# Rotary turn of queries and keys by two products and accumulating transfers, with the far scores one step later

## The chip, the cores and the metric

The kernel runs on one core of a Trainium2 chip. The metric is the device time in microseconds of one execution; the time before is the median of three runs. The profile shows one execution; its span goes from the first to the last instruction.

## The reference, cut to what matters

One decoder layer: 512 tokens, model width 1024, float32. A wide projection gives queries, keys and values for three groups of 8 heads of 64, the input of a state-space recurrence, and gate logits. Queries and keys are turned by position (rotary), then three causal attentions with different dilations run and are merged by their softmax denominators; the recurrence runs beside them, and the two are gated, projected, normalised and followed by a SwiGLU and a second normalisation.

```python
def apply_rope(t, pos):
    half = HEAD_DIM // 2                      # 32
    inv_freq = ROPE_THETA ** (-jnp.arange(half, dtype=jnp.float32) / half)
    ang = pos[:, None] * inv_freq[None, :]
    cos = jnp.cos(ang)[None, :, None, None, :]
    sin = jnp.sin(ang)[None, :, None, None, :]
    t1 = t[..., :half].astype(jnp.float32)
    t2 = t[..., half:].astype(jnp.float32)
    return jnp.concatenate([t1 * cos - t2 * sin, t1 * sin + t2 * cos], axis=-1)
...
proj = x @ w_in[layer]
q = apply_rope(q, pos)
k = apply_rope(k, pos)
for g, (window, dilation) in enumerate(((128, 1), (512, 4), (2048, 16))):
    o_g, lse_g = dilated_group_attention(q[:, :, g], k[:, :, g], v[:, :, g], window, dilation)
wts = jax.nn.softmax(jnp.stack(lses, axis=0), axis=0)
attn = jnp.sum(wts[..., None] * jnp.stack(outs, axis=0), axis=0)
```

## The kernel before

Each float32 product on TensorE (PE) is made as three products of rounded parts: both operands are split into a high and a low part, and `mm3` issues high x high, high x low and low x high (lines 202 to 204). Weights come from HBM as raw blocks of 1 MB through SP's queue; each half block is split by ACT (`whi`, line 195) and VectorE (DVE; `wlo`, line 196). The class `Weights` keeps three pairs of split buffers: after each step `w.release()` hands one back and splits the next half block into it.

The projection is a list of 56 steps (`STEPS`), each one weight half block against all 512 tokens: 24 matmuls of 128x512. The order is: the recurrence's input (steps 0 to 3), group 0's values (4 to 7), six pairs of gate tiles (8 to 19), group 0's keys (20 to 23) and queries (24 to 27), group 1's values, keys and queries (28 to 31, 32 to 35, 36 to 39), group 2's first two key tiles (40, 41), first two query tiles (42, 43), values (44 to 47), last two key tiles (48, 49), last two query tiles (50, 51), and the last four gate tiles (52 to 55). Then come the GLU of the recurrence's output (56 to 59), the branch projections (60 to 67), the output projection, the feed-forward part and the normalisations.

Other work is laid between by hand: `at_step(n, ...)` puts a function into the middle of step n (after the fourth of eight slices, through `mid`), and `n + 0.5` at its end, after `w.release()`. The engines' instruction queues are filled in exactly this order; nothing is reordered later.

A key or query step (`qk_tile`) makes one tile of 128 rows, two heads of 64, by 512 tokens. `hp` is the tile's number in its group, 0 to 3. Each tile is turned on DVE straight from PSUM: a shuffle inside each block of 32 partitions (`sw`), a product with the cosines (`cq`), a product of `sw` with the signed sines, and the sum into the tile of the group (`dv`). For this the columns of the weights are permuted on the host, so that the partner of each row lies 16 partitions away in the same block of 32. Group 0's tiles are stored with the tokens in another order (`as_phases`).

The attention is done for four pairs of heads, and twice: kind 0 (near: group 0) and kind 1 (far: groups 1 and 2 together). `SCORES[kind]` and `WEIGHTS[kind]` give the places. For pair j, `attn_scores` (PE products at line 806, then for each block a mask and row minimum on DVE, line 817, and the exponential on ACT, line 819) stands at `SCORES[kind][j]`; `attn_turn` (PE transposes of the weights at line 829 and ACT copies at line 831) at `WEIGHTS[kind][j]`; `attn_values` (line 840 and ACT's copy of the result) at `SCORES[kind][j + 1]`. The far scores of pair hp read tile hp of the queries and keys of groups 1 and 2. Functions put at the same place run in the order in which they were put there: values first, then scores.

Around the end stand `merge_sel` (52), `merge_weights` (54: the shares of the near and far kind from their row minima and sums), `split_y` (54.5: the recurrence's output split for the GLU, four casts on ACT and four differences on DVE), `merge_turn` (55.5: PE transposes of the shares), and `merge_pair(hp)` at 58 to 61. The tile pool `at` gives the tags `sw` and `cq` two buffers of 512 floats each; besides the turn, the recurrence's GELU (`y2`), the GLU's gate (`th`) and the merged pair (`a1`) use them. PSUM banks: projection tiles go round banks 0 to 2, scores and turned weights round 3 to 6, values use 7.

POOL (GpSimd) has only memsets and some work of the normalisations; before the change it issues no transfer at all.

Of the kernel before, what the change touches and what calls it, by code (L numbers as in the profile page):

```python
# [10 lines left out]
F32 = mybir.dt.float32  # L11
# [3 lines left out]
ALU = mybir.AluOpType  # L15

P = 128
# [6 lines left out]
NH = 8  # L24
# [21 lines left out]
NLAST = 4  # L46


SCORES = [[30, 33.5, 37, 40, 43.5], [43.5, 48.5, 51.5, 53, 55.5]]
WEIGHTS = [[32, 35.5, 38.5, 42], [45, 50, 52.5, 54]]  # L50

# [3 lines left out]
def by_phase(z):  # L57
    return z.rearrange("p (r c) -> p r c", r=4)


def as_phases(z):

    return z.rearrange("p (c r) -> p r c", r=4)
# [35 lines left out]
class Weights:  # L99
# [58 lines left out]
    def flush(self):  # L158
        if self.after:
            self.after()  # L160
            self.after = None
# [6 lines left out]
def emit(ctx, tc, i, out):  # L168
    nc = tc.nc
    pe, dve, act, pool, sp = nc.tensor, nc.vector, nc.scalar, nc.gpsimd, nc.sync  # L170
# [47 lines left out]
    at = pa_ctx.enter_context(tc.tile_pool(name="at", bufs=2))  # L218
# [12 lines left out]
    def gat(n, name, dt=F32):  # L231
        return pa.tile([P, 2048], dt, tag=f"gat{n}", name=name)
# [4 lines left out]
    w = Weights(nc, wp, split)  # L237
    out_homes = deque(("g0", 2, 6, 3))
    w.add(None, 8)
    for n in range(2, N_GLU, 2):  # L240
        kind, g, un, _ = STEPS[n]
# [61 lines left out]
    rope = pr.tile([P, 2, 512], F32, tag="rope", name="rope")  # L303
# [23 lines left out]
    def ts(o, a, s1, op0, s2=None, op1=None, eng=dve):  # L327
        if s2 is None:
            eng.tensor_scalar(o, a, s1, None, op0=op0)
        else:  # L330
            eng.tensor_scalar(o, a, s1, s2, op0=op0, op1=op1)

    def stt(o, a, s1, b, op0, op1, eng=dve):
        eng.scalar_tensor_tensor(o, a, s1, b, op0=op0, op1=op1)

    def tt(o, a, b, op, eng=dve):
        eng.tensor_tensor(o, a, b, op=op)  # L337
# [196 lines left out]
    ssm = {}  # L534
# [165 lines left out]
    def ssm_out(rnd):  # L700

        if rnd == 0:
            late.take(1000)
            ssm["ysb"] = gat(0, "ysb").rearrange("p (a i b c) -> p a i b c", a=2, i=4, b=2)
        ut, h, y = ssm["ut"], ssm["h"], ssm["ysb"]
        tb, cb = ([ring_(f"y{n}{rnd}{e}").rearrange("p (o i c) -> p o i c", o=2, i=2) for e in range(2)]
                  for ring_, n in ((scores, "t"), (turned, "c")))
        for e in range(2):
            for par in range(2):
                for half, rows in halves64:  # L710
                    for x, cols in halves64:
                        i_ = 4 * rnd + 2 * e + x
                        pe.matmul(tb[half][cols, par, e], ssm["tm"][rows, 2 * i_ + par, :], ut[rows, 2 * i_ + par, :],
                                  start=True, stop=True)
        for e in range(2):
            for half in range(2):
                for r in range(2):
                    for par, rows in halves64:
                        for x, cols in halves64:
                            i_ = 4 * rnd + 2 * e + x  # L720
                            pe.matmul(cb[par][cols, half, e], caf[rows, i_, r, half, :], h[r][rows, 2 * i_ + half, :],
                                      start=(r == 0), stop=(r == 1))
        is_ = slice(2 * rnd, 2 * rnd + 2)
        yf = [y[:, half, is_].rearrange("p i b c -> p (i b c)") for half in range(2)]
        y2 = [at.tile([P, 512], F32, tag="sw", name=f"y2_{rnd}{half}") for half in range(2)]
        for half in range(2):
            for par in range(2):
                act.copy(y[:, half, is_, par], tb[half][:, par])
                tt(y[:, half, is_, par], y[:, half, is_, par], cb[par][:, half], ALU.add)
        for a, b in zip(y2, yf):  # L730
            act.square(a, b)
            ts(a, a, 0.044715, ALU.mult, 1.0, ALU.add)
            tt(a, a, b, ALU.mult)
        for a, b in zip(y2, yf):
            act.activation(a, a, AF.Tanh, scale=math.sqrt(2.0 / math.pi))
            stt(b, a, 1.0, b, ALU.add, ALU.mult)
# [17 lines left out]

    def qk_tile(dv, ws, g, hp, name, mid):
        b = proj_tile(ws, f"p{name}{hp}", mid)
        sw = at.tile([P, 512], F32, tag="sw", name=f"sw{name}{hp}")
        cq = at.tile([P, 512], F32, tag="cq", name=f"cq{name}{hp}")
        dve.stream_shuffle(sw, b, list(range(16, 32)) + list(range(16)))
        tt(cq, b, rope[:, 0, :], ALU.mult)  # L760
        tt(sw, sw, rope[:, 1, :], ALU.mult)
        if g == 0:
            tt(as_phases(dv[:, hp, :]), by_phase(cq), by_phase(sw), ALU.add)
        else:
            tt(dv[:, hp, :], cq, sw, ALU.add)

    def v_tiles(dv, ws, j, g, mid):

# [81 lines left out]
    merged = {}  # L850
# [46 lines left out]
    def merge_pair(hp):  # L897
        if hp == 0:
            for j, n in (("g1", "h"), (1, "l")):
                merged[n] = home(j, f"at{n}", F32R).rearrange("p (q t) -> p q t", q=4)  # L900
        wb = [pairs_(f"wb{hp}{k}") for k in range(2)]
        for kind in range(2):
            pe.matmul(wb[kind], merged["sel"][:, kind, hp, :], merged["w"], start=True, stop=True)
        tt(oa[1][:, hp, :], oa[1][:, hp, :], wb[1], ALU.mult)
        a1 = at.tile([P, 512], F32, tag="cq", name=f"a1{hp}")
        tt(a1, oa[0][:, hp, :], wb[0], ALU.mult)
        tt(a1, a1, oa[1][:, hp, :], ALU.add)
        hi, lo = merged["h"][:, hp, :], merged["l"][:, hp, :]
        act.copy(hi, a1)
        pending.append(lambda: tt(lo, a1, hi.bitcast(F32), ALU.subtract))  # L910
# [64 lines left out]
    for kind in range(2):  # L975
        for j, n in enumerate(SCORES[kind]):
            if j > 0:
                at_step(n, attn_values, kind, j - 1)
            if j < NPAIR:
                at_step(n, attn_scores, kind, j)  # L980
                at_step(WEIGHTS[kind][j], attn_turn, kind, j)
    xn = []
# [34 lines left out]
    for n in range(4, N_GLU):  # L1017
        kind, g, un, c = STEPS[n]
# [6 lines left out]
        else:  # L1025
            if un == 0 and c == 0:
                dv = home({"k": (1, "g3", "g0"), "q": (8, 2, 1), "v": (3, "g1", 0)}[kind][g], f"{kind}{g}")
# [3 lines left out]
            dv = qkv[g]["qkv".index(kind)]  # L1031
# [10 lines left out]
    for n in range(4):  # L1042
        ws = w.views[N_GLU + n]
        bs = []
        for e in range(2):
            b = glu(f"gl{n}{e}")
            co = slice(128 * e, 128 * e + 128)
            for k in range(4):
                mm3(b, (ws[0][:, k, co], ws[1][:, k, co]), (gluin["y"][0][:, k, :], gluin["y"][1][:, k, :]), k == 0, k == 3)
            bs.append(b)  # L1050
        th = at.tile([P, 512], F32, tag="sw", name=f"th{n}")
        act.activation(th, bs[1], AF.Tanh, scale=0.5)
        stt(th, th, 1.0, bs[0], ALU.add, ALU.mult)
        flush()
        split(gh_[:, n, :], gl_[:, n, :], th, 0.5)
        w.release()
        run_fill(N_GLU + n)
        run_fill(N_GLU + n + 0.5)
# [368 lines left out]
    for t in range(NTT - 1):  # L1427
        z, bst, mv = hn[t], bsts[t], mvs[t]
# [22 lines left out]
def constants():  # L1451
    f32 = np.float32
    half = 32
    inv = (f32(10000.0) ** (-np.arange(half, dtype=f32) / f32(half))).astype(f32)
    ang = (TOKENS.astype(f32)[:, None] * inv[None, :]).astype(f32).astype(np.float64)
    p = np.arange(P)
    fr = ((p % 64) // 32) * 16 + p % 16
    sgn = np.where((p % 32) >= 16, 1.0, -1.0)
    cos = np.cos(ang).astype(f32).T[fr]
    sin = (np.sin(ang).astype(f32).T[fr] * sgn[:, None]).astype(f32)  # L1460
    rope = np.stack([cos, sin], 1)
    order = np.arange(P)
    q, j = order[:, None], order[None, :]
    near = np.concatenate([j >= q, j <= q], 1)
    order = TOKENS[:P] // 4
    q, j = order[:, None], order[None, :]
    far = np.concatenate([j <= q, (j <= q) & ((q - j) % 4 == 0)], 1)
    masks = np.stack([near, far], 1)
    masks = np.where(masks, f32(0.0), f32(NEG)).astype(f32)
    return {"rope": rope, "masks": masks, "ident": np.eye(P, dtype=f32)}  # L1470


def layout(a):
    x = a["x"][0][TOKENS]
    w = a["w_in"][0]
    hd = np.concatenate([np.arange(0, 16), np.arange(32, 48), np.arange(16, 32), np.arange(48, 64)])
    perm = (np.arange(NH)[:, None] * 64 + hd[None, :]).reshape(-1)
    parts = [w[:, 4608:5120]]
    for g in range(3):
        parts.append(w[:, 1536 + 512 * g : 1536 + 512 * g + 512][:, perm])  # L1480
        parts.append(w[:, 512 * g : 512 * g + 512][:, perm])
        parts.append(w[:, 3072 + 512 * g : 3072 + 512 * g + 512])
    parts.append(w[:, 5120:])

# [14 lines left out]
    parts = [units(p, 4, 512) if j in (0, 3, 6, 9) else pairs(p, 8, P) for j, p in enumerate(parts)]  # L1499
# [49 lines left out]
```

## Time and profile before

| | |
|---|---|
| median of 3 runs | 838.9 us (838.74 to 838.99) |
| profiled execution | 838.9 us, span 836.9 us, granted clock 0.998 |
| PE busy | 827.2 us (99%) |
| DVE busy | 589.8 us (70%) |
| ACT busy | 357.5 us (43%) |
| POOL busy | 25.8 us (3%) |
| transfers | 94.33 MB, 113 GB/s on average |

The busy shares say how much of the span an engine works, the chain says which engine's work ended last at each time, and the list of waits says who waited for whom, for how long in all, how often, and the longest. In a timeline a row begins with its start and its length in microseconds; matmuls overlap, so the distance of two starts, and not the length, is the time that one takes. In the table by stretches each engine has its busy time with the number of instructions, in the order PE, PE's weight loads, DVE, ACT, POOL, then the granted clock, the share of the transfer engines and GB/s.

### The profile page before, as it was taken

The page shows a single profiled execution, that of the slowest core. Times are in us where ns is not written, and L with a number is a line of the kernel's source. Part 1 is how long each engine was busy: PE and PEld are TensorE (multiplying, and loading weights), DVE is VectorE, ACT ScalarE, POOL GpSimd, SP SyncE. Part 2 cuts the span into 40 slices and gives each one's busy share as a digit, 9 for nine tenths or more (in the row PEclk, how much of TensorE's full clock was granted, in tenths as well). Part 3 has the DMA queues.
Part 4 walks back from the last instruction along what each step waited for, and adds up shares of the span by engine and source line. Part 5 has one row for each costly group of instructions (what it writes and reads, how often), then busy time and mean ns, then how long its engine had stood idle before and what let it go on. Part 6 is the DMA issues. An engine that isn't in the chain of part 4 may idle for free.

```text
span 836.9 us, 12834 instructions
## 1 busy us (share of the span) xinstructions
PE 827.2 (99%) x5296; PEld 723.7 (86%) x5296; DVE 589.8 (70%) x1027; ACT 357.5 (43%) x541; POOL 25.8 (3%) x27
## 2 busy tenths in 40 slices
PE   9999999999999999999999999999999999999996
PEld 7888888888888888888888899999999999888885
DVE  7976899973666526546886699888888888533337
ACT  6863332245444434644233354444455455422211
POOL 0000000000000000000000420000000000000005
PEclk9999999999999999999999999999999999999999
DMA  9732421335222222212624153233333212722203
GB/s 335 191 107 105 126 101 51 107 105 151 92 71 81 69 87 70 83 51 101 246 76 182 51 174 128 101 103 105 118 116 114 102 51 101 297 85 85 88 1 100
DMA packets 24729, 94.33 MB, mean 113 GB/s; under 512 B 6368, under 2 KB 11232, under 8 KB 15072
## 3 DMA queue, kind: packets, MB, share of 16 engines
q1 hardware_dynamic: 23040, 91.83, 32.0%
q10 hardware_dynamic: 1632, 1.70, 0.6%
q8 instruction: 41, 0.67, 0.3%
q14 instruction: 16, 0.13, 0.0%
HBM read 86.97 MB, written 6.55 MB: 112 GB/s over the span
## 4 chain that ended last, share of the span: by engine, by line
PE 98%; DVE 1%; DMA 1%; issue 0%; ACT 0%; SPq 0%; DVEq 0%
PE dn L203 5%; PE dn L202 5%; PE dn L204 5%; PE pg L202 4%; PE pg L204 3%; PE pg L203 3%; PE pv L202 3%; PE pk L202 3%; PE pq L202 3%; PE pv L203 3%; PE pq L204 3%; PE pv L204 3%; PE pk L204 3%; PE pq L203 3%; PE pk L203 3%; PE pu L602 2%
## 5 line engine op out<-in xcount | busy, mean ns | idle before, releaser
L196 DVE TENSOR_TENSOR wlo<-raw,whi 128x1024 fp32r<-128x1024 f32 x94 | 115.1, 1227 | 117.2 <-ACT whi L195 117.2
L195 ACT CAST whi<-raw 128x1024 fp32r<-128x1024 f32 x94 | 98.2, 1048 | 160.6 <-PE dn L204 63.5
L1264 ACT CAST whi<-sums 128x1024 fp32r<-128x1024 f32 x40 | 42.0, 1050 | 95.6 <-DVE sums L337 95.6
L202 PE MATMUL dn<-whi,ffh 128*128 128x512 f32 x168 | 65.4, 389 | 0.0
L203 PE MATMUL dn<-wlo,ffh 128*128 128x512 f32 x168 | 65.4, 389 | 0.0
L204 PE MATMUL dn<-whi,ffl 128*128 128x512 f32 x168 | 65.4, 389 | 0.0
L202 PE MATMUL pg<-x_hi,whi 128*128 128x512 f32 x128 | 50.5, 395 | 0.0
L204 PE MATMUL pg<-x_hi,wlo 128*128 128x512 f32 x128 | 49.9, 390 | 0.0
L203 PE MATMUL pg<-x_lo,whi 128*128 128x512 f32 x128 | 49.9, 390 | 0.0
L337 DVE TENSOR_TENSOR wlo<-sums,whi 128x1024 fp32r<-128x1024 f32 x40 | 48.7, 1220 | 0.0
L202 PE MATMUL pq<-x_hi,whi 128*128 128x512 f32 x96 | 37.9, 395 | 0.0
L202 PE MATMUL pk<-x_hi,whi 128*128 128x512 f32 x96 | 37.8, 394 | 0.0
L204 PE MATMUL pq<-x_hi,wlo 128*128 128x512 f32 x96 | 37.4, 390 | 0.0
L204 PE MATMUL pk<-x_hi,wlo 128*128 128x512 f32 x96 | 37.4, 390 | 0.0
L203 PE MATMUL pk<-x_lo,whi 128*128 128x512 f32 x96 | 37.4, 390 | 0.0
L203 PE MATMUL pq<-x_lo,whi 128*128 128x512 f32 x96 | 37.4, 389 | 0.0
L202 PEld LDWEIGHTS dn<-whi,ffh 128*128 128x128 f32 x168 | 31.6, 188 | 6.6
L204 PEld LDWEIGHTS dn<-whi,ffl 128*128 128x128 f32 x168 | 31.5, 188 | 6.6
L203 PEld LDWEIGHTS dn<-wlo,ffh 128*128 128x128 f32 x168 | 31.6, 188 | 6.4
L819 ACT ACTIVATE un<-un,st 128x256 f32<-128x256 f32 (+1 forms) x64 | 30.8, 483 | 11.0 <-DVE st L817 11.0
L919 ACT ACTIVATE gt<-pg,bgate 128x512 f32<-128x512 f32 x16 | 11.0, 689 | 46.4 <-PE pg L204 46.4
L202 PEld LDWEIGHTS pg<-x_hi,whi 128*128 128x128 f32 x128 | 24.0, 188 | 5.3 <-issue 0.2
(658 smaller groups left out, 2360.6 us busy)
## 6 DMA issues: line engine op xcount, KB each, us to landing
raw<-in_w_in SPq DMA_DIRECT2D x26, 1024.0 KB, 4.8
raw<-in_w_dn SPq DMA_DIRECT2D x11, 1024.0 KB, 4.8
ra<-in_w_gu SPq DMA_DIRECT2D x10, 1024.0 KB, 4.7
rb<-in_w_gu SPq DMA_DIRECT2D x10, 1024.0 KB, 4.9
raw<-in_w_br SPq DMA_DIRECT2D x4, 1024.0 KB, 4.8
raw<-in_w_out SPq DMA_DIRECT2D x4, 1024.0 KB, 4.7
raw_x<-in_xw SPq DMA_DIRECT2D x2, 1024.0 KB, 8.8
raw<-in_w_glu SPq DMA_DIRECT2D x2, 1024.0 KB, 4.7
```

Of the source, the lines that this page charges most:

```text
L195: act.copy(hi, src)
L196: dve.tensor_tensor(lo, src, hi.bitcast(F32), op=ALU.subtract)
L202: pe.matmul(dst, a[0], b[0], start=first, stop=False)
L203: pe.matmul(dst, a[0], b[1], start=False, stop=False)
L204: pe.matmul(dst, a[1], b[0], start=False, stop=last)
L337: eng.tensor_tensor(o, a, b, op=op)
L602: pe.matmul(bs[e][:, cs], wk[a], xk[b], start=(k + a + b + cs.start == 0), stop=(k == KT - 1 and a == 1))
L819: act.activation(pt, pt, AF.Exp, bias=mneg, scale=-1.0, accum_out=zsum)
L919: act.activation(gts[ch // 4][:, ch % 4, :], b, AF.Tanh, bias=bgate[:, ch : ch + 1], scale=0.5)
L1264: act.copy(hi, src)
```

## The change

The weights' columns stay in their order, so that the partner of a row lies 32 partitions away, in a neighbouring block of 32. A tile is turned by two products on DVE, both read from PSUM: with the cosines into the tile of the group, and with the sines (signs by the source row) into a tile `z` that holds two tiles of the group. After the second tile of such a pair POOL's queue issues four transfers that add block q ^ 1 of `z` to block q of the group's tiles (32 partitions x 2 x 512 floats each). The tags `sw` and `cq` now have one buffer of 2 x 512 floats each; `y2`, `th` and `a1` are adapted to that. The far scores of pair 0 go from 43.5 to 44.5, of pair 2 from 51.5 to 52.5, of pair 3 from 53 to 54, and the turns of pairs 0, 2 and 3 go a step later too; the values of pair 1 and 2 move with the scores that they stand beside.

```diff
-SCORES = [[30, 33.5, 37, 40, 43.5], [43.5, 48.5, 51.5, 53, 55.5]]
-WEIGHTS = [[32, 35.5, 38.5, 42], [45, 50, 52.5, 54]]
+SCORES = [[30, 33.5, 37, 40, 43.5], [44.5, 48.5, 52.5, 54, 55.5]]
+WEIGHTS = [[32, 35.5, 38.5, 42], [46, 50, 53.5, 55]]
...
-        y2 = [at.tile([P, 512], F32, tag="sw", name=f"y2_{rnd}{half}") for half in range(2)]
+        y2 = at.tile([P, 2, 512], F32, tag=("sw", "cq")[rnd], name=f"y2_{rnd}", bufs=1)
+        y2 = [y2[:, half] for half in range(2)]
...
     def qk_tile(dv, ws, g, hp, name, mid):
         b = proj_tile(ws, f"p{name}{hp}", mid)
-        sw = at.tile([P, 512], F32, tag="sw", name=f"sw{name}{hp}")
-        cq = at.tile([P, 512], F32, tag="cq", name=f"cq{name}{hp}")
-        dve.stream_shuffle(sw, b, list(range(16, 32)) + list(range(16)))
-        tt(cq, b, rope[:, 0, :], ALU.mult)
-        tt(sw, sw, rope[:, 1, :], ALU.mult)
+        if hp % 2 == 0:
+            ssm["z"] = at.tile([P, 2, 512], F32, tag=("sw", "cq")[hp // 2], name=f"z{name}{hp}", bufs=1)
+        z = ssm["z"]
         if g == 0:
-            tt(as_phases(dv[:, hp, :]), by_phase(cq), by_phase(sw), ALU.add)
+            out, rot, args = as_phases(dv[:, hp, :]), as_phases(z[:, hp % 2, :]), [by_phase(v) for v in (b, rope[:, 0, :], rope[:, 1, :])]
         else:
-            tt(dv[:, hp, :], cq, sw, ALU.add)
+            out, rot, args = dv[:, hp, :], z[:, hp % 2, :], (b, rope[:, 0, :], rope[:, 1, :])
+        tt(out, args[0], args[1], ALU.mult)
+        tt(rot, args[0], args[2], ALU.mult)
+        if hp % 2 == 1:
+            for q in range(4):
+                pool.dma_start(dv[32 * q : 32 * q + 32, hp - 1 : hp + 1, :], z[32 * (q ^ 1) : 32 * (q ^ 1) + 32], accum_op=ALU.add)
...
-        a1 = at.tile([P, 512], F32, tag="cq", name=f"a1{hp}")
+        if hp % 2 == 0:
+            flush()
+            merged["a"] = at.tile([P, 2, 512], F32, tag="cq", name=f"a1{hp}", bufs=1)
+        a1 = merged["a"][:, hp % 2]
...
-        th = at.tile([P, 512], F32, tag="sw", name=f"th{n}")
+        th = at.tile([P, 2, 512], F32, tag="sw", name=f"th{n}", bufs=1)[:, 0]
...
-    fr = ((p % 64) // 32) * 16 + p % 16
-    sgn = np.where((p % 32) >= 16, 1.0, -1.0)
+    fr = p % 32
+    sgn = np.where((p % 64) >= 32, -1.0, 1.0)
...
-        parts.append(w[:, 1536 + 512 * g : 1536 + 512 * g + 512][:, perm])
-        parts.append(w[:, 512 * g : 512 * g + 512][:, perm])
+        parts.append(w[:, 1536 + 512 * g : 1536 + 512 * g + 512])
+        parts.append(w[:, 512 * g : 512 * g + 512])
```

More of the change, by code (lines that the diff above doesn't have):

```diff
@@ L1475, in layout @@
     w = a["w_in"][0]
-    hd = np.concatenate([np.arange(0, 16), np.arange(32, 48), np.arange(16, 32), np.arange(48, 64)])
-    perm = (np.arange(NH)[:, None] * 64 + hd[None, :]).reshape(-1)
     parts = [w[:, 4608:5120]]
     for g in range(3):
-        parts.append(w[:, 1536 + 512 * g : 1536 + 512 * g + 512][:, perm])
-        parts.append(w[:, 512 * g : 512 * g + 512][:, perm])
+        parts.append(w[:, 1536 + 512 * g : 1536 + 512 * g + 512])
+        parts.append(w[:, 512 * g : 512 * g + 512])
         parts.append(w[:, 3072 + 512 * g : 3072 + 512 * g + 512])
```

## The prediction

> **What bounds the kernel now.** I read the page's busy shares first, then the chain that ended last, then PE's own waits, then a table by stretches of time.
>
> ```profile
> PE 827.2 (99%) x5296; PEld 723.7 (86%) x5296; DVE 589.8 (70%) x1027; ACT 357.5 (43%) x541; POOL 25.8 (3%) x27
> PE 98%; DVE 1%; DMA 1%; issue 0%; ACT 0%; SPq 0%; DVEq 0%
> PE warm_b L281 <- DVE warm L277: 1.1, 1, 1.1
> PE fs10x L1296 <- DVE quad L337: 0.8, 1, 0.8
> PE pu L602 <- ACT wuh L195: 0.5, 1, 0.5
> PE kb L558 <- issue: 0.5, 1, 0.5
> 10.00:166.00 156.00, 155.53 (x924) 128.88 (x923) 138.07 (x361) 70.17 (x80) 0.43 (x1) 1.00 0.41 133
> 278.00:336.00 58.00, 58.00 (x388) 48.59 (x388) 27.38 (x65) 25.28 (x56) 0.00 (x0) 1.00 0.27 90
> 336.00:372.00 36.00, 36.00 (x270) 30.49 (x269) 18.09 (x54) 22.55 (x57) 0.00 (x0) 1.00 0.18 63
> ```
>
> TensorE is the chain (98%), and its waits above are all it has: 2.9 us in four places, none at a projection tile, a score or a value product. In the two stretches that hold the far scores PE is busy 58.00 of 58.00 and 36.00 of 36.00 us, while DVE (third column after the length) is half idle. So work taken off DVE here buys nothing, and each new wait of PE is paid in full. The changed stretches have only one way to move.
>
> **The change part by part.**
>
> *DVE's products.* Each of 24 tiles loses a shuffle and a sum.
>
> ```profile
> L759 DVE STREAM_SHUFFLE swq<-pq 128x512 f32<-128x512 f32 x12 | 8.9, 742 | 0.0
> L759 DVE STREAM_SHUFFLE swk<-pk 128x512 f32<-128x512 f32 x12 | 8.9, 740 | 0.0
> L337 DVE TENSOR_TENSOR k<-cqk,swk 128x512 f32<-128x512 f32 x12 | 9.9, 824 | 0.4
> L337 DVE TENSOR_TENSOR q<-cqq,swq 128x512 f32<-128x512 f32 x12 | 9.9, 823 | 0.4
> ```
>
> Removed: 8.9 + 8.9 + 9.9 + 9.9 = 37.6 us of DVE. The remaining products keep their size; in group 0 both now write in strided phase order, for which the sums' means (824, above the 0.69 us of a plain one shown below) are the bound: under half a microsecond more for each of 16 products, some 6 us. Net about 31 us less DVE. On the path: 0, because PE waits for no such instruction; the single buffers that replace pairs of `th` and `a1` cost nothing either, since a step of 5.5 us lies between two uses and the reads are over well before.
>
> *The transfers.* New are 48 accumulating transfers from POOL's queue, four for each two tiles, each of 32 partitions x 1024 floats = 128 KB. The rotated tile is usable only when the fourth has landed. The trace has no transfer issued by POOL and none that accumulates, so both prices are bounded by neighbours.
>
> ```profile
> 33.92 3.77 SPq L620 DMA_DIRECT2D ut<-udr  x8
> L1107 POOL TENSOR_TENSOR mva<-mva,epsb 128x1 f32<-128x1 f32 x4 | 3.8, 961 | 61.3 <-DVE mva L329 61.3
> L1134 POOL TENSOR_TENSOR hn<-hn,lnb 128x512 f32<-128x512 f32 x3 | 5.6, 1867 | 0.2
> out_dram<-hr SPq DMA_DIRECT2D x12, 128.0 KB, 2.4
> ut<-udr SPq DMA_DIRECT2D x8, 128.0 KB, 4.9
> raw<-in_w_in SPq DMA_DIRECT2D x26, 1024.0 KB, 4.8
> ```
>
> Issue: from 3.77/8 = 0.47 us (SP) up to 1.87 (POOL's longest row); I take 0.96, POOL's row for an operation on almost no data, since building descriptors is overhead rather than data. Landing: 2.4 to 4.9, the two rows of 128 KB. The 2.4 is nearest (long runs), plus a second read of the destination: 1 MB takes 4.8, so 896 KB cost 2.4 us and 128 KB about 0.35; I take 2.75. Four in a row: 4 x 0.96 + 2.75 = 6.6 us from the products to the last landing (ends 4.3 and 12.4). The Trainium skill's page "DMA: Bandwidth & Descriptors", section "Anatomy of one DMA — SWDGE (gpsimd) path", speaks for the low end: a fixed 2.0 us per transfer, bytes at 436 GB/s, and descriptor generation called small; by it the four would be in after about 2.0 + 1.2 = 3.2 us (an estimate from that page) and the two terms A and B below would be 0, the sum 0.7 us (839.6). No run here shows that path yet.
>
> *A: first far pair, now half a step after step 44.* It needs tiles 0 and 1 of the group-2 queries; the second is made in step 43.
>
> ```profile
> 278.69 1.75 PE L840 MATMUL o<-un,v 128*64 128x128 f32 x28
> 280.37 2.06 PE L806 MATMUL s<-k,q 64*128 64x128 f32 x32
> 282.36 0.50 PE L202 MATMUL pv<-whi,x_hi 128*128 128x512 f32 x1
> 290.65 1.91 PE L829 MATMUL t<-ident,un 128*128 128x128 f32 x16
> 278.81 0.74 DVE L759 STREAM_SHUFFLE swq<-pq 128x512 f32<-128x512 f32 x1
> 279.44 0.67 DVE L337 TENSOR_TENSOR cqq<-pq,rope 128x512 f32<-128x512 f32 x1
> 280.04 0.68 DVE L337 TENSOR_TENSOR swq<-swq,rope 128x512 f32<-128x512 f32 x1
> 280.75 0.69 DVE L337 TENSOR_TENSOR q<-cqq,swq 128x512 f32<-128x512 f32 x1
> ```
>
> From 282.36 to 290.65 PE does a step and a half, so a step is 5.53 us. With the scores moved, step 44 starts at 280.37 and ends at 285.9. DVE starts at 278.81; two products at the spacing of the rows (0.60, then 0.68) end at 280.1. The transfers have 5.8 us and take 6.6: **late by 0.8**. A weight load of 1 MB may overlap their beginning; by the 4.8 us row it is over before the last of them.
>
> *B: third far pair, now half a step after step 52*, behind the second pair's values.
>
> ```profile
> 333.49 0.39 PE L204 MATMUL pq<-x_hi,wlo 128*128 128x512 f32 x1
> 333.81 1.97 PE L840 MATMUL o<-un,v 128*64 128x128 f32 x32
> 335.71 2.06 PE L806 MATMUL s<-k,q 64*128 64x128 f32 x32
> 333.93 0.74 DVE L759 STREAM_SHUFFLE swq<-pq 128x512 f32<-128x512 f32 x1
> ```
>
> Step 52 starts at about 333.75 and ends at 339.25; the values take 335.71 - 333.81 = 1.9, so the scores are due at 341.15. Products end at 335.2. Room 5.95, need 6.6: **late by 0.65**. The second pair (its inputs a step or more old) and all near pairs (two steps or more behind their tiles) are covered: that cover is at least 11 us against 6.6, and it fails only near the upper end of the price.
>
> *The product buffer.* In group 2 the keys' and the queries' pair use the same buffer one after the other, so DVE's second product of step 42 waits for the transfers issued after step 41, and likewise in step 50. Room about 6.3 us, so DVE may wait some 0.3 us. Behind it in DVE's queue stands only the split of a weight block that PE wants steps later: 0 on the path. POOL holds nothing else there but one memset of 0.4 us.
>
> *C: the last pair, a step later, meets the merge weights.* Scores of the fourth pair move to the middle of step 54, where the merge weights already stand; the turn moves to 55, behind the split of the recurrence's output (54.5) in ACT's queue.
>
> ```profile
> 347.88 1.97 PE L840 MATMUL o<-un,v 128*64 128x128 f32 x32
> 357.35 1.91 PE L829 MATMUL t<-ident,un 128*128 128x128 f32 x16
> 359.02 0.47 PE L202 MATMUL pg<-x_hi,whi 128*128 128x512 f32 x1
> 355.42 0.19 ACT L819 ACTIVATION_READ_ACCUMULATOR un<-un,st 128x1 f32 x1
> 358.05 2.05 ACT L831 COPY un<-t 128x512 f32<-128x512 f32 x4 [0.93 <-PE t L829]
> 359.96 0.29 ACT L879 ACTIVATE dm<-dm 128x64 f32<-128x64 f32 x1
> 361.48 0.24 ACT L886 CAST wt<-dm 128x64 fp32r<-128x64 f32 x1 [1.23 <-DVE dm L337]
> 363.59 2.19 ACT L198 ACTIVATE yh<-ych 128x512 fp32r<-128x512 f32 x4
> ```
>
> Let M be the start of the values and scores in the middle of a step (347.88 before). The last exponential ends at 355.61 = M + 7.7. Then three small DVE operations (about 0.55), the weights' exponential at M + 8.3, their cast 1.52 later, done at M + 10.1, a gate and a weight cast (together what lies between the cast's end and the split, from 361.72 to 363.59 less a wait, some 1.55), the split's four casts (2.19): M + 13.8. Only then the four copies of the turned weights, 0.51 each: the last at M + 15.9. PE turns at M + 9.5, has half a step (2.85) left at M + 11.1, and wants the values at M + 14.0; following the copies block by block it ends at M + 16.4 instead of 15.9: **0.5**. If ACT comes out of it early it is 0.
>
> *D: more switches.* The first pair's scores no longer stand next to the values, so PE goes once more from projection to attention and back. Before, 333.49 to 333.81 is 0.32 where two projection matmuls start 0.23 apart, and a step and a half takes 8.29 for 36 starts of 0.227 = 8.16: **0.2**.
>
> Sum: 0.8 + 0.65 + 0.5 + 0.2 = 2.15 us. The profiled execution took 838.9 us, 2.0 more than its span of 836.9, and its time is the median of the three (838.74 to 838.99). Forecast 838.9 + 2.15 = **841.1 us**, 0.26% slower. About 0.2% (1.7 us) is what separates a difference from none here.
>
> **The rivals.**
>
> *The transfers are in time* (the other side). POOL issues at SP's 0.47 us and they land in 2.4: 4.3 us against rooms of 5.8 and 5.95. A and B are 0, C and D stay: 0.7, so 839.6, no measurable change. The point that decides is a need under about 5.8 us. For it: POOL is idle in the whole stretch, and DMA engines are busy 0.27 and 0.18 of it. Against: POOL's smallest real operation already costs twice SP's issue. The Trainium skill's page "DMA: Bandwidth & Descriptors", in the section named above, is on this side.
>
> *Late by several microseconds.* Either the landing is 4.9 (need 8.75: A 2.95, B 2.8) or the issue is 1.87 (need 10.2: A 4.4, B 4.3). With C and D that is 6.45 and 9.4 more: 845.4 or 848.3; both together (12.4: 6.6 + 6.45 + 0.7) 852.7. For it: accumulation reads two blocks and writes one, and the source and destination are neighbours. Against: 128 KB is a small part of what a 1 MB load moves in 4.8.
>
> *Faster.* It would need a wait on PE that DVE's 31 us shorten. The list of waits has only 0.8 us on DVE at line 1296, far behind the change: at most 838.1, still within 0.2%; a true gain needs something the profile does not show.
>
> **How the numbers follow.** Late by a little (total 1.7 to 5 us more): 0.40. In time: 0.40, nearly all of it within 0.2%. Late by more than 5: 0.15. Faster: 0.05. Slower by over 0.2% is 0.40 + 0.15, less a little where A and B come out small: 0.52; within 0.2%: 0.43; faster: 0.05. The range goes from 838.6 (in time, C hidden) to 847.0, which leaves out the upper half of the late cases and the gain; the forecast's own range is 840.6 to 844.
>
> **What would show it.** DVE's busy time near 559 and no shuffle. In the list of waits, PE at line 806's scores waiting for transfers into `q` twice, near 286 and 342, 0.5 to 1 us each; if these rows are missing, A and B are wrong. PE at line 840 waiting for ACT's copies of `un` once near 373, at most 1 us; if missing, C is wrong. Issues by POOL about 1 us apart, landing in 2.5 to 3. The prediction fails if POOL's issue costs half or twice the row I took, or if PE loses time at places that none of these steps names, such as an engine slowed by the transfers.

## The result and the profile after

The changed kernel takes 840.93 us (median of 12 runs, 840.55 to 841.39) against 838.9 for the kernel before (12 runs, 838.59 to 839.12): a ratio of 1.0025 [1.0016, 1.0034], a quarter of a per cent slower and clear of the noise. The profiled execution shown below took 841.21 us with a span of 839.3; before it was 838.9 and 836.9. So its own difference is 2.3 us where the medians differ by 2.0, and the ledger below is a ledger of the 2.3.

The page of the kernel after: busy times, the queue that is new, the chain of work that ended last, and all waits of PE (us in total, times, longest). Line 810 is the scores' line (806 before), line 1303 was 1296.

```profile
PE 828.5 (99%) x5296; PEld 724.0 (86%) x5296; DVE 561.7 (67%) x955; ACT 357.3 (43%) x541; POOL 63.7 (8%) x75
q0 software_dynamic: 2304, 6.29, 5.8%
PE 93%; DVE 3%; DMA 2%; ACT 1%; issue 0%; POOL 0%; SPq 0%; DVEq 0%; ACTq 0%
...
PE warm_b L281 <- DVE warm L277: 1.1, 1, 1.1
PE fs10x L1303 <- DVE quad L337: 0.8, 1, 0.8
PE pu L602 <- ACT wuh L195: 0.8, 1, 0.8
PE s L810 <- DMA q<-zq: 0.5, 1, 0.5
PE kb L558 <- issue: 0.3, 1, 0.3
PE fs1z L1303 <- DVE hl L196: 0.2, 1, 0.2
```

DVE did lose its 28.1 us (589.8 to 561.7; its sums and shuffles are gone), and PE, still the bound, gained nothing from it. Two waits are new: the scores on the transfers into `q`, and a small one at `fs1z`, far from the change. DMA holds 2% of the chain, where it held 1% before.

The groups of DVE's products and POOL's issues (line, engine, operation, out<-in, count | busy, mean ns | idle before, releaser), and the issues with KB each and median us to landing:

```profile
L337 DVE TENSOR_TENSOR q<-pq,rope 128x512 f32<-128x512 f32 x12 | 9.9, 827 | 35.8 <-PE pq L204 35.8
L337 DVE TENSOR_TENSOR zq<-pq,rope 128x512 f32<-128x512 f32 x12 | 9.7, 811 | 0.6 <-DMA k<-zk 0.6
L769 POOL DMA_DIRECT2D k<-zk x24 | 19.0, 1212 | 246.0 <-DMA raw<-in_w_in 137.9 <-DVE zk L337 69.5 <-PE o L844 38.6
L769 POOL DMA_DIRECT2D q<-zq x24 | 18.9, 1206 | 54.7 <-DVE zq L337 45.6 <-PE o L844 9.1
...
q<-zq POOLq DMA_DIRECT2D x24, 128.0 KB, 4.1
```

The products cost what the sums had cost (0.81 to 0.83 us). POOL is busy 0.79 us per issue (18.9 / 24): the entries of four issues in a row begin 0.50 us apart and end 0.79 apart. The transfers land 4.1 us after their issue (median), not 2.75. The two late places, from the order of time (start, us, line, operation, count [idle before]):

```profile
279.48 0.68 DVE L337 TENSOR_TENSOR zq<-pq,rope 128x512 f32<-128x512 f32 x1
280.68 3.14 POOL L769 DMA_DIRECT2D q<-zq  x4 [9.10 <-PE o L844]
286.12 0.71 PE L810 MATMUL s<-k,q 64*128 64x128 f32 x6
287.30 1.80 PE L810 MATMUL s<-k,q 64*128 64x128 f32 x26 [0.46 <-DMA q<-zq]
289.02 0.50 PE L202 MATMUL pv<-whi,x_hi 128*128 128x512 f32 x1
...
336.74 3.14 POOL L769 DMA_DIRECT2D q<-zq  x4 [9.54 <-DVE zq L337]
342.38 2.65 PE L810 MATMUL s<-k,q 64*128 64x128 f32 x32
344.96 0.50 PE L202 MATMUL pg<-x_hi,whi 128*128 128x512 f32 x1
```

The 32 score products, to the next block's first matmul, take 289.02 - 286.12 = 2.90 us where they took 282.36 - 280.37 = 1.99 before: 0.91 lost. The wait's own row shows 0.46 of it; six products run before it, and the modelled end of a product hides the rest, so starts of blocks are the better measure. At the other place it is 344.96 - 342.38 = 2.58 against 1.98 (337.69 - 335.71): 0.60 lost, and the list of waits has no row for it at all. The chain in order of time has it: at both places it runs through the last of the four transfers, 4.99 us from 282.18 and 4.87 from 338.23.

The ledger of PE's block starts, after less before, each at the first matmul of the block if nothing else is said:

| block | before | after | late by | added here |
|---|---|---|---|---|
| values beside step 43's end | 278.69 | 278.76 | 0.07 | |
| first key tile after the first far scores | 306.05 | 307.28 | 1.23 | scores 0.91, one more switch 0.26 (rounded) |
| second far pair | 313.48 | 314.71 | 1.23 | 0 |
| GLU's first product (third and last pair over) | 369.71 | 371.55 | 1.84 | scores 0.60, last pair 0 |
| `fs1y` | 509.78 | 511.62 | 1.84 | 0 |
| `fs1z`, its second matmul | 512.77 | 514.97 | 2.20 | 0.36 |
| last product `dq` | 823.88 | 826.09 | 2.21 | 0 |
| end of the span | 836.9 | 839.3 | 2.4 | 0.2, at the program's end |

### The profile page after: what moved, and what is told of

It is laid out like the page before. It is cut to its first block, busy times and chain, and to the rows that moved or that the text cites. A ratio compares the mean times of both kernels' runs of the same rounds, so it can differ in the third digit from the quotient of the medians.

```text
span 839.3 us, 12913 instructions
## 1 busy us (share of the span) xinstructions
PE 828.5 (99%) x5296; PEld 724.0 (86%) x5296; DVE 561.7 (67%) x955; ACT 357.3 (43%) x541; POOL 63.7 (8%) x75
## 4 chain that ended last, share of the span: by engine, by line
PE 93%; DVE 3%; DMA 2%; ACT 1%; issue 0%; POOL 0%; SPq 0%; DVEq 0%; ACTq 0%
PE dn L204 5%; PE dn L203 5%; PE dn L202 5%; PE pg L202 3%; PE pg L203 3%; PE pg L204 3%; PE pk L202 3%; PE pq L202 3%; PE pq L204 3%; PE pk L204 3%; PE pq L203 3%; PE pk L203 3%; PE pv L202 2%; PE pv L204 2%; PE pv L203 2%; PE pu L602 2%
## 5 line engine op out<-in xcount | busy, mean ns | idle before, releaser
L769 POOL DMA_DIRECT2D k<-zk x24 | 19.0, 1212 | 246.0 <-DMA raw<-in_w_in 137.9
L337 DVE TENSOR_TENSOR q<-pq,rope 128x512 f32<-128x512 f32 x12 | 9.9, 827 | 35.8 <-PE pq L204 35.8
```

Of the source, the lines that this page charges most:

```text
L769: pool.dma_start(dv[32 * q : 32 * q + 32, hp - 1 : hp + 1, :], z[32 * (q ^ 1) : 32 * (q ^ 1) + 32], accum_op=ALU.add)
```

## The experiments

The theory, from this trace: PE pays for two landings that come a little late (A, B) and for one more switch (D); the last pair (C) is free; a small part is elsewhere. The rivals: the moved places cost by themselves; the transfers slow PE or other engines wherever they run; the time lies in the transfers' number, not in their lateness.

**The two halves apart.** First the places alone, with the turn as before:

```diff
 # before.py, with
+SCORES = [[30, 33.5, 37, 40, 43.5], [44.5, 48.5, 52.5, 54, 55.5]]
+WEIGHTS = [[32, 35.5, 38.5, 42], [46, 50, 53.5, 55]]
```

> The turn of before (shuffle, two products, sum) with the later places of the far scores and turns: the schedule alone. Theory (the loss is two waits for transfers, A about 0.9 and B about 0.6, plus one more switch between projection and attention, D about 0.25): 839.2, no wait at the scores. Rival 1 (the later places themselves cost, by the crowded queue of ACT at the end, as my term C had it): 839.7 to 840. Rival 2 (the whole loss comes from moving the scores): 840.9.

838.94 us (838.6 to 839.36) against 838.62: 1.0003 [0.9995, 1.0012]. By the medians the moved places cost 0.3 us or nothing that can be told from it. The block starts tell it: PE is 0.27 us ahead of the kernel before at the values beside step 43's end (278.42) and 0.02 ahead at the first key tile behind the far scores (306.02), so D is 0.25, and nothing is lost behind that. The last pair's scores, turn and values stand here exactly where the change puts them, and PE's whole list of waits is:

```profile
PE warm_b L281 <- DVE warm L277: 1.1, 1, 1.1
PE fs10x L1296 <- DVE quad L337: 0.8, 1, 0.8
```

No copy by ACT is waited for: C does not exist. Then the turn alone, with the far scores at their old places:

```diff
 # after.py, with
+SCORES = [[30, 33.5, 37, 40, 43.5], [43.5, 48.5, 51.5, 53, 55.5]]
+WEIGHTS = [[32, 35.5, 38.5, 42], [45, 50, 52.5, 54]]
```

> The new turn with the places of before, so that the scores of pairs 0 and 2 follow their tile at once. Theory: PE waits for the four transfers almost in full, at pair 0 some 6.9 us (landing about 7.1 us after the products, PE ready 0.3 us after them) and at pair 2 some 6.3 us; D is gone: 838.9 + 13 = 852. Rival (the transfers are only a little late anyway, the step of room is not needed): under 842.

855.64 us (855.13 to 856.03): 1.0201 [1.0187, 1.0215], slower by 17 us, 3.6 more than expected. Its list of waits, the first far pair, and two stretches of it:

```profile
PE s L810 <- DMA q<-zq: 10.6, 4, 4.5
...
279.94 0.49 PE L810 MATMUL s<-k,q 64*128 64x128 f32 x4
280.18 3.14 POOL L769 DMA_DIRECT2D q<-zq  x4 [9.11 <-PE o L844]
284.94 0.76 PE L810 MATMUL s<-k,q 64*128 64x128 f32 x2 [4.51 <-DMA q<-zq]
286.84 3.32 PE L810 MATMUL s<-k,q 64*128 64x128 f32 x26 [1.13 <-DMA q<-zq]
290.09 0.79 PE L202 MATMUL pv<-whi,x_hi 128*128 128x512 f32 x1
...
279.94:290.09 10.15, 4.50 (x34) 3.85 (x33) 2.65 (x10) 2.05 (x7) 3.14 (x4) 0.61 0.44 56
290.09:292.50 2.41, 2.41 (x7) 1.93 (x7) 1.23 (x8) 2.41 (x12) 0.00 (x0) 0.50 0.00 0
```

Here nothing covers the transfers: 290.09 - 279.94 = 10.15 us for a block of 1.99, 8.2 lost, and 7.5 in the same way at 344.59. Not all of it is the wait for the transfers, as the two stretches show, which have the granted clock in the third place from the end. In the middle of each of the two long waits the granted clock falls to 0.50, from 282.26 for 10.2 us and from 347.11 for 6.8 us. The 26 products behind the waits take 3.25 and 3.20 us, where the changed kernel takes 1.72 for them at a clock of 1.00, and the step and a half behind the first pair are 1.15 us longer than before, 4.2 us in all. Without that the two blocks lose 6.6 and 6.0 us, close to the 6.9 and 6.3 expected; the slower clock is what the expectation left out. The later place of the scores is thus worth 15.7 - 1.5 = 14 us to this turn, the slower clock included; without it the change would lose eight times as much. What the change costs is small only because the readers were moved with it.

**The transfers that are waited for, taken out.** Group 2's queries keep only their product with the cosines: the eight transfers that add the part with the sines are left out.

```diff
-        if hp % 2 == 1:
+        if hp % 2 == 1 and name != "q2":
```

> The changed kernel without the eight accumulating transfers of group 2's queries, so these queries lack their sine part (part of the computation is left out). Theory: only these transfers were waited for, so A and B vanish and D stays: 839.2 to 839.5. Rival (transfers slow PE or other engines in general, by traffic or by POOL's work; 40 of 48 remain): 840.5 or more.

838.77 us (838.44 to 839.52): 1.0003 [0.9994, 1.0011]. The other 40 transfers stay, near pairs and keys alike, and cost nothing: the first far block takes 1.98 us again, there is no wait at the scores, and PE's list is

```profile
PE warm_b L281 <- DVE warm L277: 1.1, 1, 1.1
PE fs10x L1303 <- DVE quad L337: 0.8, 1, 0.8
PE kb L558 <- issue: 0.3, 1, 0.3
```

So nearly the whole loss hangs on eight of the 48 transfers, and the rival by which transfers slow PE wherever they run falls. The 1.5 us of the two waits are the greater part of it; the 0.36 us at `fs1z` and a part of the 0.2 at the program's end go as well in this kernel; both come up again below.

**The same transfers earlier.** Each tile sends its own four transfers of 64 KB right after its products, so that the first tile of each pair goes a step earlier; 96 in all.

```diff
-        if hp % 2 == 1:
-            for q in range(4):
-                pool.dma_start(dv[32*q : 32*q + 32, hp - 1 : hp + 1, :], z[32*(q ^ 1) : 32*(q ^ 1) + 32], accum_op=ALU.add)
+        for q in range(4):
+            pool.dma_start(dv[32*q : 32*q + 32, hp, :], z[32*(q ^ 1) : 32*(q ^ 1) + 32, hp % 2], accum_op=ALU.add)
```

> The changed kernel, but each tile is followed by its own four transfers of 64 KB (96 in all) instead of four of 128 KB after two tiles. The scores of pairs 0 and 2 read tiles 0 and 2, whose transfers now start a step (5.5 us) earlier. Theory: A and B vanish, twice the issues cost nothing since POOL is idle: 839.2 to 839.5. Rival (what counts is the number of issues or the traffic): 841 or more.

842.73 us (842.42 to 843.21): 1.005 [1.0036, 1.0064]. Slower than the change, against my expectation, though the wait is gone as expected. Its waits, its scores, its last product on PE and its last output:

```profile
PE warm_b L281 <- DVE warm L277: 1.1, 1, 1.1
PE fs10x L1302 <- DVE quad L337: 0.8, 1, 0.8
PE pu L602 <- ACT wuh L195: 0.2, 1, 0.2
...
285.30 2.06 PE L809 MATMUL s<-k,q 64*128 64x128 f32 x32
287.29 0.50 PE L202 MATMUL pv<-whi,x_hi 128*128 128x512 f32 x1
...
823.39 0.28 PE L202 MATMUL dq<-whi,ffh 128*128 128x256 f32 x1
833.46 0.35 SPq L1454 DMA_DIRECT2D out_dram<-hr  x1
...
core 0: 840.6 us, clock 0.996
```

PE's last block starts at 823.39, half a microsecond before that of the kernel before (823.88), and the last output is issued at 833.46 against 833.95. (That lead is older than the change: at the values beside step 43's end this profile is already 0.75 us ahead, and D takes 0.25 of it.) Yet the span ends at 840.6, 3.7 us later. The lost time lies behind the last instruction that the page counts. What stands there in the trace's records is POOL's closing entry, a drain that begins with POOL's last operation and has to end before the closing exchange of the engines. Its length in the profiles so far, and how far it ends behind SP's readiness (all outputs in):

| kernel | transfers issued by POOL | drain, us | its end behind SP's readiness, us |
|---|---|---|---|
| before, places only | 0 | 1.09 | -3.8 |
| the transfers of group 2's queries left out | 40 | 4.38 | -0.6 |
| after | 48 | 5.03 | +0.1 |
| each tile its own | 96 | 8.95 | +4.0 |

(8.95 - 1.09) / 96 = 0.082 us for each transfer that POOL issued, wherever in the program it stood. SP's last outputs hide the first 4.9 us of it, so that only the last two rows show it in the span.

**The drain by itself.** If that reading is right, transfers that nobody waits for must cost the same. The kernel before, with 96 POOL transfers of 8 bytes per partition into a spare tile, three in each of 32 steps, on 16 partitions and on 128 (the rival: the cost goes by rows, not by transfers):

```diff
+    scr = sa.tile([P, 96, 2], F32, name="scr")
+    def dummy(j):
+        for e in range(3):
+            pool.dma_start(scr[0:16, 3 * j + e, :], i["ident"][0:16, 0:2])   # 0:128 in the second
+    for j in range(32):
+        at_step(6 + j, dummy, j)
```

> The kernel before, with 96 small transfers added on POOL's queue (16 partitions x 8 bytes each, from a constant into a tile that nothing reads, three at the middle of each of steps 6 to 37). They touch nothing that anybody waits for. Theory (each transfer that POOL issues lengthens the drain at the end of POOL's program by 82 ns, as 5029 ns with 48 and 8949 ns with 96 suggest; SP's end hides the first 4.9 us): drain about 8.9 us, 842.7. Rival 1 (the last run's loss came from the traffic or the accumulation): 838.6. Rival 2 (the drain goes by rows, not by transfers; half as many rows here as in the per-tile kernel): drain about 5 us, 838.9.

> The same with 128 partitions x 8 bytes per transfer, eight times the rows. Theory (the drain goes by the number of transfers): again about 8.9 us, 842.7. Rival (it goes by rows): far longer, 30 us or more, over 860.

842.52 us (842.38 to 842.9) and 843.01 (842.74 to 843.44) against 838.68: 1.0047 [1.0033, 1.006] and 1.0052 [1.004, 1.0065]. The 16-row kernel's group of issues:

```profile
L1010 POOL DMA_DIRECT2D scr<-in_ident x96 | 46.2, 487 | 14.7 <-DMA scr<-in_ident 12.7 <-issue 1.3
```

PE's list of waits has the two rows of the places alone and no other, and the drains take 8.94 and 8.95 us, ending 4.03 us behind SP in both. With eight times the rows, and 64 KB accumulated in place of 128 bytes, the drain stays at 8.95: it goes by the number of transfers. 3.8 and 4.3 us of loss are the drain's 4.0 within the intervals.

**Order and number set against each other.** Only group 2's queries by the tile (56 transfers in all), first each tile at once, then both after the second tile with the tile that is needed last at the end:

```diff
-        if hp % 2 == 1:
+        if name == "q2":                           # second kernel: and hp % 2 == 1
+            for h in (hp,):                        # second kernel: (hp, hp - 1)
+                for q in range(4):
+                    pool.dma_start(dv[32*q : 32*q + 32, h, :], z[32*(q ^ 1) : 32*(q ^ 1) + 32, h % 2], accum_op=ALU.add)
+        elif hp % 2 == 1:
```

> The changed kernel, with transfers per tile for group 2's queries alone (16 instead of 8, 56 in all), each right after its tile. Theory: A and B vanish as in the per-tile kernel, D (0.25) stays, and the drain with 56 transfers is 5.7 us, 0.8 over what SP's end hides: 839.7. Rival (the drain is no matter, A and B are all): 838.9.

> As the run before, but both tiles' transfers after the second tile, with the tile that the scores need first issued last: 56 transfers. Theory (the path is POOL's wake-up 0.5, then 0.785 us per issue, then the landing): four more issues stand before the needed ones and their bytes are halved, so the scores of pairs 0 and 2 wait about 2.8 us each; with D and 0.8 for the drain 845. Rival (landing by bytes alone sets the wait, since the bytes before the last landing are the same): as the changed kernel plus 0.8, 841.5.

839.56 us (839.17 to 840.3), 1.001 [1.0002, 1.0019], and 845.6 (844.7 to 845.78), 1.0078 [1.0066, 1.0091]. The first has no wait at the scores; its drain of 5.68 us ends 0.8 us behind SP's readiness, and D is 0.24 in its profile: together 1.0 for the 0.9 us that it loses. It is the best version with all of the turn done by transfers, and not faster than before. The second kernel shows what the queue's order costs:

```profile
PE s L814 <- DMA q<-zq: 3.3, 4, 1.1
...
280.23 6.32 POOL L770 DMA_DIRECT2D q<-zq  x8 [9.11 <-PE o L848]
288.36 1.80 PE L814 MATMUL s<-k,q 64*128 64x128 f32 x26 [1.01 <-DMA q<-zq]
345.95 3.32 PE L814 MATMUL s<-k,q 64*128 64x128 f32 x26 [1.10 <-DMA q<-zq]
```

Eight issues in 6.32 us again are 0.79 each. The same bytes in eight pieces, the needed ones last, make the products wait 3.3 us by the list of waits. By the starts of blocks the first far pair loses 2.4 us (290.09 - 285.67, less 1.99) and the third 3.8 (349.20 - 343.45, less 1.98). The 26 products of the last row take 3.25 us to the next block, since the granted clock is 0.50 from 345.93 to 349.34; 1.5 of the 3.8 us are that.

**The small wait at `fs1z`.** The changed kernel once more, unaltered, for a second profile:

> The changed kernel once more, unaltered, for one more profile. In the first profile PE lost 0.36 us at the start of the second GLU product's successor (the matmul into fs1z, some 514 us, where DVE had paused 0.46 us), far from the change. If that is noise of the one profile, the wait of fs1z on DVE is missing here and the products into dn start within 0.2 of 711.47 (1.85 after before's 709.62). If it belongs to the change, the row stands again with 0.2 us and dn starts near 711.8. Either way the scores wait near 287 by 0.4 to 0.6 us, and POOL's end lasts 5.03 us.

```profile
PE s L810 <- DMA q<-zq: 0.6, 1, 0.6
PE fs1z L1303 <- DVE hl L196: 0.2, 1, 0.2
...
512.98 0.69 DVE L337 TENSOR_TENSOR ff<-fth,fg 128x512 f32<-128x512 f32 x1 [0.46 <-DVE fth L334]
711.72 0.40 PE L202 MATMUL dn<-whi,ffh 128*128 128x512 f32 x1
```

It took 841.1 us (one run). The row stands again, and `dn` starts 2.10 us after the kernel before (709.62): not noise. DVE stands idle for 0.46 us ahead of this operation: from the start of the one before it are 1.14 us (511.84 to 512.98) where all others have 0.79 (before: 510.09 to 510.88), 0.35 more. It shows in both profiles of the changed kernel and in the turn alone, which has as many DVE instructions (1119, waits for semaphores counted), and in none of the seven other kernels or in the one before, which have 1115 or 1121 to 1165. One thing in the trace's records goes with it. In the three profiles with the pause a transfer of 8 KB of instructions, on the queue q14, starts 0.67 to 0.68 us after the paused operation does (513.76 in the first profile of the changed kernel); in the others none on this queue starts within a microsecond of the operation. That points to the loading of DVE's instructions, but no run sets it apart, so the cause stays open; PE loses 0.36 us by the pause.

## Why the prediction was right

841.1 was forecast and 840.93 measured, on the expected side. Term by term it was less exact than that: one term was nothing, and two that were not in the sum, 0.36 and 0.2 us, filled its place. That the total came within 0.2 us is luck to that extent; that PE pays for two late landings, at the places and about in the sizes named, is not.

- **DVE's 31 us less buy nothing: right.** DVE's busy time fell by 28.1. The products in phase order cost about what was taken: a mean of 1.07 us in the trace where a plain one has 0.69, some 6.5 us more for the sixteen. In the changed stretches DVE holds one link of the chain, the product `zq` ahead of the transfers of the third pair (0.69 us at 335.76), and nothing that was taken off it was waited for.
- **A, 0.8: measured 0.91. B, 0.65: measured 0.60.** The mechanism and both places are those named. The price of 6.6 us was 7.0, from the end of the products (280.16) to the last landing (287.16), but it is made up otherwise. The first issue begins 0.52 us after the products end, which the sum did not have; the fourth begins 1.50 after the first, where the sum had four times 0.96 ahead of the last landing; and the last landing takes 4.99 us, not 2.75. My sum gave all four the same landing time. In fact they landed 3.14, 4.03, 4.42 and 4.99 us after their issues began, each later than the one before it. The row I turned down, 4.9 us for SP's 128 KB, is what the last one came to.
- **D, 0.2: 0.26 in the ledger, 0.25 with the places alone.**
- **The product buffer, some 0.3 us of DVE at two places: right.** DVE waited twice, 0.6 us in all (the row of `zq` above), and PE lost nothing by it.
- **C, 0.5: nothing.** The step that failed is the order of DVE and ACT at the merge weights. I put three small DVE operations behind the last exponential. They need only the row minima, not the exponentials' sums:

```profile
361.25 0.19 DVE L337 TENSOR_TENSOR mg<-near_st,st 128x32 f32<-128x32 f32 x1
362.70 0.19 ACT L823 ACTIVATION_READ_ACCUMULATOR un<-un,st 128x1 f32 x1
362.80 0.24 ACT L883 ACTIVATE dm<-dm 128x64 f32<-128x64 f32 x1
368.04 2.03 ACT L835 COPY un<-t 128x512 f32<-128x512 f32 x4
369.24 1.97 PE L844 MATMUL o<-un,v 128*64 128x128 f32 x32
371.14 0.66 PE L896 MATMUL wt<-ident,wt 128*128 128x128 f32 x4
```

  They ran at 361.25, while ACT still had three exponentials before it, so the weights' exponential followed the last accumulator read (362.70 to 362.89) without a gap, at M + 7.63 (M = 355.17) instead of M + 8.3, and everything behind it came at least 0.7 us sooner. The last copy ends at 370.07 = M + 14.9 instead of M + 15.9, and the values, begun at 369.24, take 371.14 - 369.24 = 1.90 us as before (369.30 - 367.40). A margin of half a microsecond on a chain of eight links needed the link's inputs looked up in the code, not its place in the text.
- **The terms that were missing:** 0.2 us at the program's end, of which 0.14 come since POOL's drain grew from 1.09 to 5.03 us and passed SP's readiness, and 0.07 since two of POOL's entries behind it are longer (0.10 and 0.14 us for 0.08 and 0.10); and 0.36 us at `fs1z`, whose cause is open. The prediction had looked at POOL's issues and landings and nowhere at what POOL does once the work is over, because there was no such transfer to show it.
- **The signs named:** POOL's issues, forecast about 1 us apart and landing in 2.5 to 3, end 0.79 us apart and land in 3.1 to 5.0; two waits of the scores on `q` were promised, and one has a row while the other is only in the starts of the blocks; the wait at line 840 for ACT is missing, which is the sign given for C being wrong. The last sign, that PE loses time at a place that no step names, came true at `fs1z`: in that 0.36 us the prediction fails by its own words.
- **"In time"** had a chance of 0.40 and did not come. Its 4.3 us, from SP's rows, stand against 7.0 us here: the issues of one row were busy 4 x 0.79 us, and each 128 KB transfer landed in 3.1 to 5.0 us. By the Trainium skill's page "DMA: Bandwidth & Descriptors", section "Anatomy of one DMA — SWDGE (gpsimd) path", which calls descriptor generation small, it would have been 3.2 us for the four and 2.3 for one transfer of 128 KB (estimates from its fit); this case's trace agrees with neither. "Late by several us" was only the turn alone, without the later places. Nothing was faster.

## What to carry to other kernels

On a kernel that one engine bounds, work taken off another engine is worth nothing, and the chain of small steps that replaces it is worth its latency up to the first reader: find that reader and count from the last input to the last landing, with the transfers of one group queued behind each other. Move the readers together with such a change (14 us here, 4 of them because the granted clock halved in the long waits) or, for the transfers that somebody is about to read, start each piece as soon as its own input is there (the best variant). And count what an engine has issued until the end of the program: a cost that stands behind the last visible instruction is seen by comparing the last output's issue with the end of the span.

## What the runs showed of the hardware beyond that

- POOL's closing drain lasts 1.09 us and 0.082 us more for each transfer that POOL issued in the whole program (40: 4.38; 48: 5.03; 56: 5.68; 96: 8.95), the same for 16 rows of 8 bytes, 128 rows of 8 bytes, and 32 rows of 2 KB accumulated. Here SP's last outputs hide the first 4.9 us, about 46 transfers.
- POOL is busy 0.79 us per accumulating transfer of 32 partitions, for 64 KB and 128 KB alike, and 0.49 (16 rows) to 0.54 us (128 rows) is the mean length of an issue of the tiny copies.
- How long such a transfer took to land went with what else was in flight. With each tile its own, 37 of the 96 transfers of 64 KB had a 1 MB weight load beside them for 4.8 us or more and landed 5.4 to 7.5 us after their issue; the other 59 took 2.4 to 4.6. At the two late places of the changed kernel the weight load landed within 0.6 us of the first issue (281.20 against 280.68, 337.18 against 336.74), so the 3.1 to 5.0 us there are the price with hardly any of it.
- With the turn alone, in the two long waits of PE (4.5 and 3.9 us in order of time), the granted clock fell to 0.50, and it stayed there for 10.2 and 6.8 us, into the work behind. In the changed kernel, whose one listed wait on a transfer is 0.5 us, it stayed at 1.00 until PE's work was over. With the needed tile last it fell for 3.4 us at waits of 0.45 and 1.10 us, and not at 0.74 and 1.01.
